# MLP of an encoder: TensorE takes pieces of the second product and half-size products of the first two and two in turn instead of one and one

## The chip, the core and the metric

The kernel runs on one core of a Trainium2 chip. The metric is the device time of one execution, in microseconds; the median of three runs of the kernel before is 1327.92 us (1327.11 to 1327.92). Engines are named as the profile names them: PE is the matrix engine (PEld its loading of weights), DVE the vector engine, ACT the scalar engine, POOL the general engine, SP the one that issues most transfers.

## What is computed

Two layers of an encoder over 512 tokens of 1024 features, in float32. Each layer is a token mixer (a gated delta rule in the first, gated linear attention in the second), a residual layer norm, and then the MLP, which the change is about:

```python
def _sq_relu_mlp(h, w1, w2):
    a = jax.nn.relu(jnp.matmul(h, w1))
    return jnp.matmul(a * a, w2)

x = _layernorm(DEEPNORM_ALPHA * x + m.astype(x.dtype), ln1_g[i], ln1_b[i])
x = _layernorm(DEEPNORM_ALPHA * x + _sq_relu_mlp(x, mlp_w1[i], mlp_w2[i]).astype(x.dtype), ln2_g[i], ln2_b[i])
```

`w1` is 1024 x 4096 and `w2` 4096 x 1024.

## The kernel before

**Arithmetic.** A float32 operand is split into a high part (`h`: a cast on ACT, line 102) and the rest (`l`: a subtraction on DVE, line 107). One product of two tiles is then three matmuls, high by high, high by rest and rest by high (`mm3`, lines 125 to 130). Both products of the MLP use a Winograd form of Strassen's scheme, with seven products of half size in place of eight, and sums of quarters around them.

**The loops.** `mlp` goes over the 4096 hidden features in four groups. While PE works on the second product of group `gi` (`second`, line 564), it also works out the first product of group `gi + 1` (`stream`, line 740). There are three such stretches in each of the two MLPs, six in all.

- A **piece** is a quarter of one of the seven products in `second`: six matmuls of 128x512 into one of the banks pX, pY, pZ (`chunks`, line 544). There are 28 in a stretch, `i` = 0 to 27.
- A **half-size product** belongs to a pair of hidden features (`Pair`, line 450): twelve matmuls of 128x256. A pair has seven, four pairs (`p` = 0 to 3) make 28 in a stretch.

The seven of a pair stand in the order of `products` (line 491), named here by the bank that they write and the number of the product: X1, Z2, X6, Y5, X7, Y3, X4. X is the tile `fx`; Z and Y are the two halves of the tile `fyz`. X is written four times by one pair, and each time its content has to be taken out first: after X1 by ACT (line 499), after X6 by ACT (505), after X7 by DVE (511), after X4 by ACT (520). X4 adds to X, so it waits for line 511 of its pair.

**Weights of a pair.** Its tiles `wh` and `wl` come from rings of three buffers. `prepare(i + 1)`, called when Y5 of pair `i` has been issued (line 749), makes on DVE what products 1, 2 and 5 of the next pair need: a split (ACT 102, DVE 107) in the buffer that Y5 gives back, five sums (DVE, line 464), and a split of half a tile (ACT 470, DVE 471) in the buffer that Y3 gives back. `late` makes the other two splits.

**What sets the order.** On PE the order is that in which the code issues (`in_order`, line 765). On ACT and DVE the framework's scheduler decides at build time, by durations of its own, in which order the instructions of all these helpers stand; on the chip each of these queues is a fixed list, and an instruction that waits holds up those behind it.

The loop that mixes the two kinds is lines 766 to 769: after piece `i` PE takes half-size products until `i + 1` of them have been issued, so one after each piece. In the last stretch of an MLP (`m = 24`), whose pieces 24 to 27 are left for the end, all that is left of the 28 follows piece 23.

Of the kernel before, what the change touches and what calls it, by code (L numbers as in the profile page):

```python
# [351 lines left out]
def mlp(c, w1, w2, g, b, out=None, extra=None, room=0):  # L352
# [14 lines left out]
    with c.banks(pj=2, X=2, Y=2, Z=2), tc.tile_pool(name="mlp", bufs=2) as pool:  # L367
# [51 lines left out]
        def new_h():  # L419
            return [pool.tile([P, HF, S], F32, name="h", tag="h", bufs=3) for _ in range(2)]  # L420
# [143 lines left out]
        def second(gi, h, a):  # L564

            a11, a12, a21, a22 = quarters(h)
            tags = "ZX" if gi + 2 == G else "XZ"
            X, Y, Z = banks(tags[0]), banks("Y"), None
            load(gi, 1, 0)

            def upto(i):

                if i == 5:
                    V.tensor_tensor(a21, a22, a21, ALU.subtract)
                elif i == 6:
                    V.scalar_tensor_tensor(a11, a21, -1.0, a11, ALU.mult, ALU.subtract)
                elif i == 7:
                    V.scalar_tensor_tensor(a21, a11, -1.0, a22, ALU.mult, ALU.subtract)
                elif i == 3:
                    V.scalar_tensor_tensor(a12, a12, -1.0, a11, ALU.mult, ALU.subtract)  # L580
                b = pair({2: a12, 5: a21, 6: a11, 7: a21, 3: a12, 4: a22}[i])
                split(i)
                return b

            steps = ((1, 2, 0, 0, ALU.add, None), (2, 5, 0, 0, ALU.add, None), (5, 6, 2, 1, ALU.subtract, None),
                     (6, 7, 0, 1, ALU.subtract, (0, 0)), (7, 3, 2, 1, ALU.subtract, (0, 1)),
                     (3, 4, 0, 1, ALU.subtract, (1, 1)), (4, None, 2, 0, ALU.add, None))
            for i, nx, t, hf, op, more in steps:
                if i == 2:
                    Z = banks(tags[1])  # L590
                bk = Z if i == 2 else Y if i in (5, 3) else X
                for n, _ in enumerate(chunks(bk, a, i, i in (1, 2, 5))):
                    if n == 0 and nx:
                        b = upto(nx)
                    if n == 3:
                        for j in range(2):
                            add(t + j, hf, bk[j], op)
                        if more:
                            load(gi + 1, *more)
                    yield  # L600
                a = b
# [138 lines left out]
        def stream(gi, nh):  # L740

            for p in range(GF // 2):
                i = (gi - 1) * (GF // 2) + p
                for n, _ in enumerate(ready[i].products(nh)):
                    if n == 0:
                        begin(i + 1)
                    elif n == 1:
                        ready[i].late(1, (7, 3))
                    elif n == 3:
                        prepare(i + 1)  # L750
                    elif n == 5:
                        finish(i + 1)
                    if p == 3 and n == 2 and gi + 1 == G:
                        load(gi, 1, 0, c.wst)
                    if p == 3 and n == 2:
                        split(1, None if gi + 1 < G else True)
                        stream.a = pair(quarters(nh)[0])
                    yield

        for gi in range(G - 1):  # L760
            nh = new_h()
            more = stream(gi + 1, nh)
            n, k = 28, 0
            m = 24 if gi + 2 == G else 28
            with c.in_order(mybir.EngineType.PE):
                for i, _ in enumerate(second(gi, h, a)):
                    while k < n and (k < i + 1 or i + 1 == m):
                        next(more, None)
                        k += 1
                for _ in more:  # L770
                    pass
            h, a = nh, stream.a
# [1040 lines left out]
def body(tc, nc, a, out):  # L1813
    with contextlib.ExitStack() as es:
        def pool(name, bufs, **kw):
            return es.enter_context(tc.tile_pool(name=name, bufs=bufs, **kw))

        c = Ctx(tc, nc, (pool("const", 1), pool("big", 1), pool("wst", 3), pool("whl", 3), pool("small", 4)))
        x = a["x"][0]
        gdn(c, (a["a_in"], a["a_gates"]), a["a_conv"][0], a["a_alog"][0], a["a_dt_bias"][0], a["a_norm_g"][0],  # L1820
            a["a_out"], a["ln1_g"][0], a["ln1_b"][0], x, a["xt"], a["w1_0"])
        with tc.tile_pool(name="gcst", bufs=1) as gp:
            gc = []
            mlp(c, a["w1_0"], a["w2_0"], a["ln2_g"][0], a["ln2_b"][0],
                room=32, extra=lambda tmp: gc.append(GlaConst(c, gp, a["b_gate_b"][0], a["b_norm_g"][0], tmp)))
            gla(c, gc[0], (a["b_in"], a["b_vr"], a["b_gates"]), a["b_gate_w2"][0], a["b_out"], a["ln1_g"][1], a["ln1_b"][1], a["w1_1"])
        mlp(c, a["w1_1"], a["w2_1"], a["ln2_g"][1], a["ln2_b"][1], out=out[0])
# [18 lines left out]
```

## Time and profile before

| | us |
|---|---|
| median of three runs | 1327.92 |
| the profiled execution | 1328.52 |
| span of its trace, first to last instruction | 1326.6 |
| PE busy | 1307.4 |
| DVE busy | 1107.7 |
| ACT busy | 805.2 |
| POOL busy | 124.8 |

The stretches in which pieces and half-size products take turns lie at about 467 to 696 us and 1042 to 1271 us of the span. In the quoted rows of a timeline the columns are start, duration, engine, line, operation, out<-in by the program's names, shape, and in brackets how long the engine had been idle before it and what ended that. Start-to-start distances, not durations, say how fast an engine works through its list, since the end of one instruction overlaps the start of the next.

### The profile page before, as it was taken

How to read it: one execution, taken by the hardware profiler on the slowest of the kernel's cores; microseconds unless marked ns; L12 is line 12 of the kernel's file. 1: busy time of each engine (PE TensorE's matmuls, PEld its weight loads, DVE VectorE, ACT ScalarE, POOL GpSimd, SP SyncE). 2: the span in 40 equal slices, each digit the busy share in tenths (PEclk: the TensorE clock that was granted, in tenths of full speed). 3: DMA queues.
4: the chain of work that ended last, by engine and by line, in shares of the span. 5: the costliest groups of instructions: out<-in, count | busy, mean ns of one | idle time of the engine just before them, and what ended most of it. 6: DMA issues, size and time to landing. Idle time of an engine off the chain costs nothing.

```text
span 1326.6 us, 22309 instructions
## 1 busy us (share of the span) xinstructions
PE 1307.4 (99%) x8659; PEld 1113.2 (84%) x8659; DVE 1107.7 (83%) x1823; ACT 805.2 (61%) x1598; POOL 124.8 (9%) x177
## 2 busy tenths in 40 slices
PE   9999999999999999999999999999999999999996
PEld 7777877787777889999998888888889889999985
DVE  7787888888668988989988787967879789989887
ACT  4757666767643666566667754654456466666656
POOL 5000000000000910101102200000001001101021
PEclk9999999999999999999999999999999999999998
DMA  5210120211222585675648521111216465657465
GB/s 181 96 49 33 49 65 33 64 49 57 73 99 85 189 178 154 156 191 153 151 150 170 149 90 64 65 63 64 95 64 213 105 193 154 149 172 161 142 143 143
DMA packets 44045, 154.36 MB, mean 116 GB/s; under 512 B 5419, under 2 KB 5795, under 8 KB 43939
## 3 DMA queue, kind: packets, MB, share of 16 engines
q1 hardware_dynamic: 32163, 110.85, 24.9%
q0 software_dynamic: 11776, 42.08, 16.1%
q8 instruction: 68, 1.11, 0.3%
q14 instruction: 38, 0.31, 0.1%
HBM read 113.99 MB, written 2.10 MB: 88 GB/s over the span
## 4 chain that ended last, share of the span: by engine, by line
PE 92%; ACT 3%; DVE 3%; issue 1%; DVEq 0%; POOL 0%; ACTq 0%; POOLq 0%
PE fx L128 3%; PE fx L130 3%; PE fx L129 3%; PE pX L130 3%; PE pX L129 3%; PE pX L128 3%; PE pjv L128 3%; PE pjv L129 3%; PE pjv L130 3%; PE m L1708 3%; PE fyz L128 3%; PE fyz L129 3%; PE fyz L130 3%; PE pY L129 2%; PE pY L128 2%; PE pY L130 2%
## 5 line engine op out<-in xcount | busy, mean ns | idle before, releaser
L102 ACT CAST wh<-wst 128x1024 fp32r<-128x1024 f32 x152 | 159.4, 1049 | 110.3 <-PE fyz L129 35.3
L107 DVE TENSOR_TENSOR wl<-wst,wh 128x1024 fp32r<-128x1024 f32 x150 | 184.3, 1229 | 42.2 <-ACT wh L102 41.9
L107 DVE TENSOR_TENSOR w2l<-w2r,w2h 128x1024 fp32r<-128x1024 f32 x92 | 112.3, 1221 | 24.0 <-ACT w2h L102 23.8
L102 ACT CAST w2h<-w2r 128x1024 fp32r<-128x1024 f32 x94 | 98.5, 1048 | 47.4 <-PE pX L130 16.2
L415 POOL DMA_DIRECT2D w2r<-w2r x56 | 48.5, 892 | 493.9 <-DVE w2l L107 247.3
L102 ACT CAST ah<-h 128x1024 fp32r<-128x1024 f32 x56 | 58.9, 1052 | 40.8 <-PE pX L129 18.1
L464 DVE TENSOR_TENSOR wst<-wst 128x512 f32<-128x512 f32 x120 | 79.8, 685 | 0.4
L107 DVE TENSOR_TENSOR al<-h,ah 128x1024 fp32r<-128x1024 f32 x56 | 68.3, 1220 | 5.1 <-ACT ah L102 4.8
L130 PE MATMUL pX<-w2h,al 128*128 128x512 f32 x168 | 66.2, 394 | 0.0
L129 PE MATMUL pX<-w2l,ah 128*128 128x512 f32 x168 | 66.1, 393 | 0.0
L128 PE MATMUL pX<-w2h,ah 128*128 128x512 f32 x168 | 65.8, 392 | 0.0
L128 PE MATMUL pjv<-wh,xth 128*128 128x512 f32 x128 | 54.7, 427 | 0.0
L128 PE MATMUL fx<-xth,wh 128*128 128x256 f32 x192 | 53.6, 279 | 0.0
L130 PE MATMUL fx<-xh,wl 128*128 128x256 f32 x192 | 53.6, 279 | 0.0
L130 PE MATMUL fyz<-xh,wl 128*128 128x256 f32 x192 | 53.6, 279 | 0.0
L128 PE MATMUL fyz<-xh,wh 128*128 128x256 f32 x192 | 53.6, 279 | 0.0
L128 PE MATMUL fx<-xh,wh 128*128 128x256 f32 x192 | 53.5, 278 | 0.0
L129 PE MATMUL fx<-xl,wh 128*128 128x256 f32 x192 | 53.5, 278 | 0.0
L130 PE MATMUL fx<-xth,wl 128*128 128x256 f32 x192 | 53.4, 278 | 0.0
L129 PE MATMUL fx<-xtl,wh 128*128 128x256 f32 x192 | 53.4, 278 | 0.0
L129 PE MATMUL fyz<-xl,wh 128*128 128x256 f32 x192 | 53.4, 278 | 0.0
L129 PE MATMUL pj<-xtl,wh 128*128 128x256 f32 (+1 forms) x160 | 52.0, 326 | 0.2 <-DVE xtl L194 0.2
(538 smaller groups left out, 4320.7 us busy)
## 6 DMA issues: line engine op xcount, KB each, us to landing
wst<-in_w SPq DMA_DIRECT2D x68, 512.0 KB, 4.3
w2r<-in_w SPq DMA_DIRECT2D x60, 512.0 KB, 4.0
w2r<-w2r POOLq DMA_DIRECT2D x56, 512.0 KB, 5.3
wst<-in_a_in SPq DMA_DIRECT2D x32, 512.0 KB, 3.3
wst<-in_b_vr SPq DMA_DIRECT2D x16, 512.0 KB, 3.3
wst<-in_a_out SPq DMA_DIRECT2D x8, 512.0 KB, 3.3
wst<-in_b_in SPq DMA_DIRECT2D x8, 512.0 KB, 3.3
wst<-in_b_out SPq DMA_DIRECT2D x8, 512.0 KB, 3.3
```

Source lines behind the costliest of these rows:

```text
L102: h = nc.scalar.copy(hi, src)
L107: self.halves = h, nc.vector.tensor_tensor(lo, src, hi.bitcast(F32), ALU.subtract)
L128: mm(ps, ah, bh, start=start, stop=False, **kw)
L129: mm(ps, ah, bl, start=False, stop=False, **kw)
L130: self.last_mm = mm(ps, al, bh, start=False, stop=stop, **kw)
L415: nc.gpsimd.dma_start(blocks[a + (q,)], blocks[b + (q,)], accum_op=ALU.add)
L464: plus = lambda a, b: V.tensor_tensor(a, a, b, ALU.add)
L1708: T.matmul(ps[:, d, :], *ops(d), start=True, stop=True)
```

## The change

```diff
             with c.in_order(mybir.EngineType.PE):
                 for i, _ in enumerate(second(gi, h, a)):
-                    while k < n and (k < i + 1 or i + 1 == m):
+                    upto = n if i + 1 == m else i + 1 if i % 7 in (1, 3, 5, 6) else k
+                    while k < upto:
                         next(more, None)
                         k += 1
                 for _ in more:
```

No instruction is added or taken away. After pieces 0, 2 and 4 of every seven no half-size product follows, after 1, 3 and 5 two, after 6 one. With P for a piece, a pair stood on PE as P X1 P Z2 P X6 P Y5 P X7 P Y3 P X4, and now stands as P P X1 Z2 P P X6 Y5 P P X7 Y3 P X4. As the scheduler lays out the other engines around this, the lists of ACT and DVE change too; those of POOL and SP stay as they were.

On DVE, pair `p` = 0 of the second stretch, from the split that waits for Y5 (the first row, `wl`) to the row that takes product 3 out of Y (514). Line 511 takes X7 out of X, 464 are the sums of `prepare`, 471 is the half split that waits for Y3 through its cast on ACT, 576 to 580 are sums for `second`, `w2l` are its weights. Before:

```order
L107 TENSOR_TENSOR wl<-wst,wh 128x1024
L511 TENSOR_TENSOR h<-h,fx 128x256
L464 TENSOR_TENSOR wst<-wst 128x512
L578 SCALAR_TENSOR_TENSOR h<-h 128x4x256
L464 TENSOR_TENSOR wst<-wst 128x512 x2
L471 TENSOR_TENSOR wl<-wst,wh 128x512
L464 TENSOR_TENSOR wst<-wst 128x512 x2
L107 TENSOR_TENSOR w2l<-w2r,w2h 128x1024
L514 TENSOR_TENSOR h<-h,fyz 128x256
```

Now, with the two rows ahead of that split (in the list of before this `w2l` stood there too, and 576 further up):

```order
L107 TENSOR_TENSOR w2l<-w2r,w2h 128x1024
L576 SCALAR_TENSOR_TENSOR h<-h 128x4x256
L107 TENSOR_TENSOR wl<-wst,wh 128x1024
L578 SCALAR_TENSOR_TENSOR h<-h 128x4x256
L464 TENSOR_TENSOR wst<-wst 128x512
L107 TENSOR_TENSOR w2l<-w2r,w2h 128x1024
L464 TENSOR_TENSOR wst<-wst 128x512 x2
L471 TENSOR_TENSOR wl<-wst,wh 128x512
L464 TENSOR_TENSOR wst<-wst 128x512 x2
L511 TENSOR_TENSOR h<-h,fx 128x256
L514 TENSOR_TENSOR h<-h,fyz 128x256
```

Line 511 has moved from the place right behind the split to the place behind 471 and all five sums.

On DVE, pair `p` = 1 of the same stretch, the same section (534 and 536 add a finished piece to the residual `xt`, `al` is the rest of an operand of `second`). Before:

```order
L107 TENSOR_TENSOR wl<-wst,wh 128x1024
L536 TENSOR_TENSOR xt_5508<-xt_5508,pY 128x512
L464 TENSOR_TENSOR wst<-wst 128x512
L511 TENSOR_TENSOR h<-h,fx 128x256
L464 TENSOR_TENSOR wst<-wst 128x512 x2
L107 TENSOR_TENSOR al<-h,ah 128x1024
L464 TENSOR_TENSOR wst<-wst 128x512
L471 TENSOR_TENSOR wl<-wst,wh 128x512
```

Now:

```order
L107 TENSOR_TENSOR wl<-wst,wh 128x1024
L536 TENSOR_TENSOR xt_5508<-xt_5508,pY 128x512
L464 TENSOR_TENSOR wst<-wst 128x512
L107 TENSOR_TENSOR al<-h,ah 128x1024
L464 TENSOR_TENSOR wst<-wst 128x512 x2
L107 TENSOR_TENSOR w2l<-w2r,w2h 128x1024
L471 TENSOR_TENSOR wl<-wst,wh 128x512
L464 TENSOR_TENSOR wst<-wst 128x512 x2
L107 TENSOR_TENSOR w2l<-w2r,w2h 128x1024
L511 TENSOR_TENSOR h<-h,fx 128x256
```

Here 511 has gone from three rows behind the split to the end of the section, behind 471 and two `w2l`. The same two rearrangements stand at `p` = 0 and `p` = 1 of all six stretches (with 578 and 580 for 576 and 578, and 534 for 536, in the first of each MLP). At `p` = 2 and `p` = 3 line 511 stays ahead of 471.

## The prediction

> **What bounds the kernel now.** I read the page's head first, then the busy times of the two stretches that the change touches, then PE's list of waits there, then the timeline of one pair.
>
> ```profile
> span 1326.6 us, 22309 instructions
> PE 1307.4 (99%) x8659; PEld 1113.2 (84%) x8659; DVE 1107.7 (83%) x1823; ACT 805.2 (61%) x1598; POOL 124.8 (9%) x177
> ```
>
> PE is busy for all but 19 us. The view by windows gives for the interleaved stretch of each MLP the window, its length, and the busy time of each engine:
>
> ```profile
> 466.80:696.40 229.60, 229.60 (x1494) 207.88 (x1493) 205.61 (x255) 143.63 (x205) 20.97 (x26) 1.00 0.62 161
> 1041.60:1271.20 229.60, 229.60 (x1494) 207.86 (x1493) 205.22 (x253) 143.05 (x203) 19.30 (x23) 1.00 0.58 155
> ```
>
> PE never stops in these 459 us, and the list of PE's waits is empty for both windows. DVE is second, with 205.61 of 229.60 us, or 90%. So nothing that DVE or ACT do here costs time today, a gain can come only from PE's own pace, and a loss from anything that makes PE wait. DVE has a tenth of its time to spare, but what matters is whether one particular instruction comes in time.
>
> **PE's own pace.** One product, one piece and the next product in the timeline:
>
> ```profile
> 521.17 0.28 PE L128 MATMUL fyz<-xh,wh 128*128 128x256 f32 x1
> ...
> 522.33 0.28 PE L129 MATMUL fyz<-xl,wh 128*128 128x256 f32 x1
> 522.44 0.28 PE L130 MATMUL fyz<-xh,wl 128*128 128x256 f32 x1
> 522.57 0.39 PE L128 MATMUL pY<-w2h,ah 128*128 128x512 f32 x1
> ...
> 523.95 0.28 PE L128 MATMUL fx<-xth,wh 128*128 128x256 f32 x1
> ```
>
> From start to start a product takes 522.57 - 521.17 = 1.40 us and a piece 523.95 - 522.57 = 1.38. The step from the last matmul of a product to the piece is 0.13 us, inside the product it is 0.11 (522.33 to 522.44), so a change of kind costs 0.01 to 0.02 us. A pair had seven of them in each direction and now has four, so 6 x 24 = 144 go. At 0.02 us that is 2.9 us; the rows have two decimals, and I take 0.5. The other direction of the bound: the two neighbours of a longer run may suit each other worse. Products in this trace take between 1.37 us (546.23 to 547.60) and 1.41 (526.72 to 528.13):
>
> ```profile
> 526.72 0.28 PE L128 MATMUL fx<-xth,wh 128*128 128x256 f32 x1
> ...
> 528.13 0.40 PE L128 MATMUL pY<-w2h,ah 128*128 128x512 f32 x1
> ...
> 546.23 0.28 PE L128 MATMUL fx<-xth,wh 128*128 128x256 f32 x1
> ...
> 547.60 0.39 PE L128 MATMUL pX<-w2h,ah 128*128 128x512 f32 x1
> ```
>
> With all 168 at one end, the pace term lies between -5 us (168 x 0.03) and +2 us (168 x 0.01). I take **-0.5 us**.
>
> The Trainium skill (TensorE: Matmul & The Clock Gate, Back-to-back issue gap) gives about 216 ns from start to start for an isolated warm matmul of 512 columns, and no price for a change of size. The rows have 231 ns a matmul (1.38 us / 6), so the measurement decides; by the page the pace term would be 0 instead of -0.5.
>
> **The wait that gets shorter.** All instructions stay, so what counts is distance on PE between an instruction that fills a bank, the one that empties it, and the next one that writes it. For X1 to X6, X6 to X7 and Y5 to Y3 two pieces and a product lie between, before and now. X4 to the next pair's X1 gains a piece. X7 to X4 loses one: from P Y3 P (1.39 + 1.40 + 1.39 = 4.2 us) to Y3 P (2.8 us). In that time DVE has to run line 511. How late that is today, at `p` = 3 of the second stretch, from the piece behind Y5 on:
>
> ```profile
> 536.54 0.40 PE L128 MATMUL pX<-w2h,ah 128*128 128x512 f32 x1
> 536.62 1.05 ACT L102 CAST wh<-wst 128x1024 fp32r<-128x1024 f32 x1 [2.07 <-PE fyz L129]
> 537.70 1.23 DVE L107 TENSOR_TENSOR wl<-wst,wh 128x1024 fp32r<-128x1024 f32 x1 [1.51 <-ACT wh L102]
> 538.96 0.69 DVE L464 TENSOR_TENSOR wst<-wst 128x512 f32<-128x512 f32 x1
> 539.57 1.22 DVE L107 TENSOR_TENSOR w2l<-w2r,w2h 128x1024 fp32r<-128x1024 f32 x1
> 540.71 1.28 DVE L464 TENSOR_TENSOR wst<-wst 128x512 f32<-128x512 f32 x2
> 541.91 0.41 DVE L511 TENSOR_TENSOR h<-h,fx 128x256 f32<-128x256 f32 x1
> 542.24 0.68 DVE L464 TENSOR_TENSOR wst<-wst 128x512 f32<-128x512 f32 x1
> ...
> 543.45 0.28 PE L128 MATMUL fx<-xth,wh 128*128 128x256 f32 x1
> ```
>
> Call 536.54, the end of Y5, S. ACT starts the split at S + 0.08, DVE its half at S + 1.16; 511 ends at 542.32 and X4 starts at 543.45, so 1.1 us is to spare. The steps also give DVE's rate: 1.14 us for an instruction of 1024 columns (539.57 to 540.71), 0.60 for one of 512 (540.71 to 541.91 is two), 0.33 for 511, which itself ends after 0.41.
>
> **Working it for the new lists.** Undisturbed, X4 now starts at S + P P X7 Y3 P = 3 x 1.39 + 2 x 1.40 = S + 6.97.
>
> At **p = 1** DVE is idle when the split arrives: the rows ahead of it are released by pieces that lie before X6 and Y5. Its list from S + 1.16 to 511, as the part on the change shows it: wl 1.14, 536 0.60, 464 0.60, al 1.14, two 464 1.20, w2l 1.14, 471 0.60, two 464 1.20, w2l 1.14, then 511 with 0.41. That is 9.17, so 511 ends at S + 10.33. With some 0.06 us for the signal, X4 starts at S + 10.4 instead of 6.97: PE waits **3.4 us**.
>
> At **p = 0** the two rows ahead of the split push it back. Their chain starts with ACT's `ah`, released by the piece ahead of X6, two products before S, at about S - 2.8; DVE's `al` follows 1.08 later (as 536.62 to 537.70 above), then al, w2l and 576 take 3 x 1.14, so wl starts at S + 1.7. From there wl 1.14, 578 1.14, 464 0.60, w2l 1.14, two 464 1.20, 471 0.60, two 464 1.20, 511 0.41 are 7.43: 511 ends at S + 9.1, and PE waits **2.2 us**.
>
> A floor that does not hang on how busy DVE is: 471 stands ahead of 511 and waits for ACT 470, which waits for Y3.
>
> ```profile
> 542.19 0.62 ACT L470 CAST wh<-wst 128x512 fp32r<-128x512 f32 x1 [3.00 <-PE fyz L129]
> ...
> 542.85 0.41 DVE L514 TENSOR_TENSOR h<-h,fyz 128x256 f32<-128x256 f32 x1
> 543.18 0.68 DVE L471 TENSOR_TENSOR wl<-wst,wh 128x512 fp32r<-128x512 f32 x1
> ```
>
> Y3 is done at about S + 5.6. The cast takes 0.62, 471 0.60, two sums 1.20, 511 0.41: S + 8.5, or 1.6 us late at p = 0, and 2.7 at p = 1 with its second w2l. Before, X4 could never meet this, as 511 stood ahead of 471.
>
> At p = 2 the new list has wl, 536, 464, 536, two 464 and 511: 1.16 + 1.14 + 5 x 0.60 + 0.41 = S + 5.7, in time. At p = 3 the rows are those quoted above, 1.16 + 1.14 + 0.60, then w2l, whose cast waits for the second piece behind S (S + 2.9 and 1.1 for the cast) and so starts at S + 4.0, then 1.14 + 1.20 + 0.41: S + 6.8, just in time, where 1.1 us was to spare. The third stretch of each MLP ends with products alone, before and now.
>
> One more place: where the second stretch of an MLP follows the first, its second piece needs bank X back from the last piece of the first. The distance falls from X4 P X1 to X4 P, and that 536 stands at the end of the list of p = 3, two 464, 514, 471, 536, 464 behind 511: about S + 10.1 against S + 9.76, so 0.35 us, twice.
>
> **Sum.** 6 x (2.2 + 3.4) = 33.6, plus 0.7, minus 0.5: +33.8 us on the profiled execution's 1328.52 (its span and 1.9 us around it), which is 1362.3; that execution lies 0.6 us over the median of the runs, so against the median it is **1362 us**, 2.6% slower. Nothing later wins this back, because PE has no other wait to lose.
>
> **Rivals.**
>
> *Only PE's pace counts (faster).* If DVE ran 511 within the 2.8 us behind X7 at every pair, the change would give what the pace can give, down to -5 us and 1323. It decides for this when 471's cast and the sums end before Y3 and the following piece do, at S + 6.5. Against it stands the floor: 470 cannot start before Y3 ends, and 511 stands behind it in a list that the trace shows run strictly in turn (511 above starts at 541.91, right behind the two sums, though X7, which lies 4.2 us ahead of X4, was done at 539.3).
>
> *The stall is there but small.* If only one of the two places bites, say p = 1 alone at its floor of 2.7, the sum is 16 us less the pace: 1344. If neither does and only the shorter distance counts at p = 3, it is 1329. For it speaks only that 511 has 1.1 us to spare at its worst place today.
>
> *PE's clock falls in the longer waits.* At the end of the kernel PE stops at 1314.60 (last row's start and duration), and the granted clock, the last figure but two of a window's row, goes down:
>
> ```profile
> 1314.20 0.40 PE L130 MATMUL pX<-xh,al 128*128 128x512 f32 x1
> 1317.00:1319.00 2.00, 0.00 (x0) 0.00 (x0) 1.93 (x9) 0.50 (x2) 0.29 (x1) 0.74 1.00 219
> 1319.00:1326.00 7.00, 0.00 (x0) 0.00 (x0) 2.63 (x8) 0.00 (x0) 1.07 (x2) 0.50 0.76 282
> ```
>
> A mean of 0.74 over 1317 to 1319 means half clock from 1317.96, 3.36 us after PE stopped. The wait at p = 1 is 3.4 us by my working, at the edge. If each of the six lost the clock, and it stayed at half for as long as it took to fall, 1.7 us each or 10 us in all would come on top: 1372. The Trainium skill (TensorE: Matmul & The Clock Gate, What's actually happening) has the array at half clock after an idle window of about 3.4 us that runs freely; the row agrees. By that rule a gap of 3.4 us would have to match a window exactly, so few of the six would.
>
> **How the numbers follow.** The forecast has 0.80: two stalls per stretch of the sizes above, each within about 0.6 us, which with the pace gives 1352 to 1370. The clock case has 0.08, the small stall 0.07 (half of it under 1331, so within 0.2%), the faster rival 0.05. A difference of 0.2%, or 2.7 us, is about what a measurement can tell from none. So faster 0.05, the same 0.04, slower 0.91. The range runs from the floors with the best pace (1328.5 + 6 x 4.3 - 5 = 1349) to the clock case: 1349 to 1372.
>
> **What would show it.** In the profile after, PE's list of waits should hold one new row, fx L128 (X4) waiting for DVE h L511, 12 times, about 34 us in total, longest 3.4 to 3.5. DVE's 511 should end just before X4 starts at p = 0 and p = 1, right behind two 464 or a w2l, with 471 ahead of it. The busy time of PE's matmuls should stay within 5 us, and DVE's as it was. The prediction is wrong if that wait isn't there, if 511 overtakes 471, or if products and pieces change their pace by more than 0.03 us each.

## The result, and the profile after

The changed kernel takes **1376.36 us** (median of 4 runs, 1372.32 to 1377.61) against 1327.92 us (1327.11 to 1329.31) for the kernel before on the same chip: a ratio of 1.0358, 95% interval 1.0334 to 1.0383. It is slower, as forecast, but by 48 us and not by 34, and it lies outside the range. The profiled execution took 1377.61 us. The head of its page, and its row in the view by cores (span, mean granted clock):

```profile
span 1375.9 us, 22345 instructions
PE 1324.7 (96%) x8659; PEld 1125.9 (82%) x8659; DVE 1110.1 (81%) x1823; ACT 808.8 (59%) x1598; POOL 125.8 (9%) x177
```

```profile
core 0: 1375.9 us, clock 0.984
```

The same number of matmuls is busy for 17 us longer (1324.7 against 1307.4), and the span is 49.3 us longer. So there are two losses: PE stops, and PE runs slower. The list of PE's waits, first for 460 to 760 us, then for 1040 to 1376 (line waited for, us in total, times, longest):

```profile
PE fx L128 <- DVE h L511: 16.6, 6, 3.3
...
PE fx L128 <- DVE h L511: 16.3, 6, 3.3
```

Both lists hold this one row and no other. It is the forecast's wait, 12 times, **33.0 us**, where 33.6 was worked out. How it comes about at `p` = 1 of the first stretch, in DVE's timeline (start, duration, line, and in brackets the idle time before it):

```profile
502.45 1.22 DVE L107 TENSOR_TENSOR wl<-wst,wh 128x1024 fp32r<-128x1024 f32 x1 [2.23 <-ACT wh L102]
503.59 0.68 DVE L534 SCALAR_TENSOR_TENSOR xt<-xt,pY 128x512 f32<-128x512 f32 x1
504.19 0.68 DVE L464 TENSOR_TENSOR wst<-wst 128x512 f32<-128x512 f32 x1
504.79 1.22 DVE L107 TENSOR_TENSOR al<-h,ah 128x1024 fp32r<-128x1024 f32 x1
505.92 1.28 DVE L464 TENSOR_TENSOR wst<-wst 128x512 f32<-128x512 f32 x2
507.13 1.21 DVE L107 TENSOR_TENSOR w2l<-w2r,w2h 128x1024 fp32r<-128x1024 f32 x1
508.26 0.68 DVE L471 TENSOR_TENSOR wl<-wst,wh 128x512 fp32r<-128x512 f32 x1
508.87 1.28 DVE L464 TENSOR_TENSOR wst<-wst 128x512 f32<-128x512 f32 x2
510.07 1.21 DVE L107 TENSOR_TENSOR w2l<-w2r,w2h 128x1024 fp32r<-128x1024 f32 x1
511.21 0.41 DVE L511 TENSOR_TENSOR h<-h,fx 128x256 f32<-128x256 f32 x1
```

From `wl` on DVE has no idle time, and 511 is the twelfth instruction of that run. PE's timeline at the same place:

```profile
507.94 0.40 PE L130 MATMUL pX<-w2h,al 128*128 128x512 f32 x1
511.67 0.39 PE L128 MATMUL fx<-xth,wh 128*128 128x256 f32 x1 [3.33 <-DVE h L511]
...
512.24 0.35 PE L129 MATMUL fx<-xtl,wh 128*128 128x256 f32 x1
512.39 0.42 PE L130 MATMUL fx<-xth,wl 128*128 128x256 f32 x1
512.60 0.42 PE L128 MATMUL fx<-xth,wh 128*128 128x256 f32 x1
512.82 0.42 PE L129 MATMUL fx<-xtl,wh 128*128 128x256 f32 x1
...
514.32 0.63 PE L129 MATMUL pX<-w2l,ah 128*128 128x512 f32 x1
514.74 0.63 PE L130 MATMUL pX<-w2h,al 128*128 128x512 f32 x1
```

PE stands for 3.33 us. Then, 0.6 us after it has started again, its steps double: from 0.12 us to 0.21 and 0.22 for 256 columns, and 0.42 for 512 columns (514.32 to 514.74) where 0.23 is usual. The view by windows shows the same for both MLPs (window, its length, busy time of each engine; the last but two is the granted clock, 1.00 in both stretches before):

```profile
466.80:720.00 253.20, 236.56 (x1466) 212.41 (x1465) 203.23 (x249) 144.78 (x202) 20.08 (x24) 0.95 0.54 142
1060.00:1320.00 260.00, 243.69 (x1524) 218.58 (x1523) 209.60 (x259) 146.80 (x206) 19.33 (x23) 0.97 0.52 137
```

The trace's record of the clock has ten falls to one half ahead of the kernel's end. Nine last for 3.41 us and one for twice that. At half clock, 11 x 3.41 us less 1.2 us in which PE stood anyway cost half of their length, **18.2 us**. With the waits that is 51.2 us on a span that grew by 49.3, so the pace of PE gave back some 2 us.

The falls begin on a raster of 3.413 us, a fixed grid in time, whatever PE does at that moment. Windows laid on this raster (idle time of PE is a window's length less the first busy time):

```profile
594.22:597.64 3.42, 0.74 (x4) 0.27 (x2) 3.42 (x5) 1.04 (x1) 0.00 (x0) 1.00 0.46 151
597.64:601.05 3.41, 2.75 (x13) 2.75 (x14) 0.93 (x3) 1.26 (x3) 0.00 (x0) 0.50 0.49 159
601.05:604.46 3.41, 3.41 (x10) 2.64 (x10) 1.86 (x2) 1.96 (x3) 0.00 (x0) 0.50 0.10 16
604.46:607.88 3.42, 3.42 (x27) 3.25 (x26) 2.18 (x4) 2.27 (x3) 0.00 (x0) 1.00 0.42 143
1085.74:1089.15 3.41, 1.52 (x8) 0.91 (x6) 3.41 (x7) 0.62 (x1) 1.75 (x2) 1.00 0.51 98
1089.15:1092.57 3.42, 3.20 (x20) 2.90 (x21) 1.63 (x4) 2.86 (x5) 0.00 (x0) 1.00 1.10 210
485.00:488.41 3.41, 1.35 (x11) 1.35 (x12) 2.94 (x6) 1.01 (x2) 0.34 (x1) 1.00 1.08 204
488.41:491.82 3.41, 3.41 (x11) 2.74 (x10) 1.58 (x2) 2.37 (x4) 0.18 (x1) 0.50 0.57 108
```

A window with 2.68 us idle (594.22) is followed by half clock, and so is one with only 2.06 us idle (485.00); one with 1.89 us idle (1085.74) is not. The window at 597.64 is at half clock and has 0.66 us idle: the next is at half clock too. After a busy one (601.05) the clock is back. All six gaps at `p` = 1 lost the clock, and four of the six at `p` = 0, which are only 2.1 to 2.5 us long.

The theory to be tested had three parts: the wait comes from the place of 511 in DVE's list and from the rows put ahead of it; the slower clock comes from PE's idle time in the waits, about 2 us of a window being enough; and apart from these two the order of two and two saves some 2 us. The rivals: the shorter distance on PE makes the stall whatever the list is, and the clock falls for another reason than idleness, such as a heavier load.

### The profile page after: what moved, and what is told of

It reads as the page before. It is cut to its first block, busy times and chain, and to the rows that moved or that the text cites. A ratio compares the mean times of both kernels' runs of the same rounds, so it can differ in the third digit from the quotient of the medians.

```text
span 1375.9 us, 22345 instructions
## 1 busy us (share of the span) xinstructions
PE 1324.7 (96%) x8659; PEld 1125.9 (82%) x8659; DVE 1110.1 (81%) x1823; ACT 808.8 (59%) x1598; POOL 125.8 (9%) x177
## 3 DMA queue, kind: packets, MB, share of 16 engines
q0 software_dynamic: 11776, 42.08, 15.5%
## 5 line engine op out<-in xcount | busy, mean ns | idle before, releaser
L128 PE MATMUL fx<-xth,wh 128*128 128x256 f32 x192 | 58.8, 306 | 33.0 <-DVE h L511 33.0
L128 PEld LDWEIGHTS fx<-xth,wh 128*128 128x128 f32 x192 | 39.6, 206 | 40.0 <-DVE h L511 38.7
L130 PE MATMUL fx<-xth,wl 128*128 128x256 f32 x192 | 57.9, 301 | 0.0
L129 PE MATMUL fx<-xtl,wh 128*128 128x256 f32 x192 | 57.7, 300 | 0.0
```

The costliest lines, as they stand in the source:

```text
L128: mm(ps, ah, bh, start=start, stop=False, **kw)
L129: mm(ps, ah, bl, start=False, stop=False, **kw)
L130: self.last_mm = mm(ps, al, bh, start=False, stop=stop, **kw)
```

## The experiments

Times before are from the same chip in the same job: 1327.72 us for e1 to e4, 1328.06 for e5 to e8, 1328.24 for e9 and e10, 1327.84 for e11.

### 511 ahead again, with PE's order of two and two

In e1 the next pair's splits and sums are issued behind the sum of X7; in e2 the same is done to the kernel before.

```diff
-                    elif n == 3:
+                    elif n == 4:
                         prepare(i + 1)
```

> The changed kernel, with the next pair's splits and sums issued one place later in the program, behind the sum of X7 (L511), so that L511 stands ahead of them in DVE's list at every pair; PE's order is that of two and two. If the order of DVE's list is the cause of both the stall and the fallen clock: no row of PE waiting for L511, granted clock 1.00 in both stretches, and what is left is the gain in pace of some 2.5 us: 1325 us (1323 to 1328). If the stall comes from the shorter distance on PE between X7 and X4 whatever stands in DVE's list (X7's sum or its bank simply come too late): the 12 waits stay, at 1 us or more each, and the time is above 1345 us. If the clock falls for another reason than the idle time of PE: windows at half clock stay with no wait beside them, about 1345 us.

> The kernel before, one and one, with the same move of the splits and sums behind L511. Both theories: no wait of PE in either, so 1328 us within 2. If it is below 1326, the move alone brings what e1 gains, and the order of two and two brings nothing; if e1 is 2 us or more below this one, that is the pace of two and two.

e1 took **1324.19 us** (1323.7 to 1324.75), a ratio of 0.9973 [0.9963, 0.9983] to the kernel before: faster than both kernels. e2 took 1326.63 us (1325.94 to 1327.29), 0.9993 [0.9984, 1.0001], which isn't told apart from no change. DVE's timeline of e1 at the place shown above:

```profile
497.37 1.23 DVE L107 TENSOR_TENSOR wl<-wst,wh 128x1024 fp32r<-128x1024 f32 x1 [2.23 <-ACT wh L102]
498.51 0.68 DVE L534 SCALAR_TENSOR_TENSOR xt<-xt,pY 128x512 f32<-128x512 f32 x1
499.11 1.22 DVE L107 TENSOR_TENSOR al<-h,ah 128x1024 fp32r<-128x1024 f32 x1
500.24 1.22 DVE L107 TENSOR_TENSOR w2l<-w2r,w2h 128x1024 fp32r<-128x1024 f32 x1
501.38 0.42 DVE L511 TENSOR_TENSOR h<-h,fx 128x256 f32<-128x256 f32 x1
501.71 0.69 DVE L464 TENSOR_TENSOR wst<-wst 128x512 f32<-128x512 f32 x1
```

Five sums, 471 and a `w2l` now stand behind 511, which ends 4.43 us after `wl` began and not 9.17. The windows of both MLPs:

```profile
466.80:720.00 253.20, 253.20 (x1604) 227.66 (x1603) 225.91 (x277) 160.13 (x225) 26.22 (x32) 1.00 0.64 163
1040.00:1320.00 280.00, 270.74 (x1678) 241.50 (x1676) 247.76 (x332) 176.40 (x271) 30.15 (x37) 0.99 0.60 154
```

PE never stops in the first; in the second it stops only at the kernel's end, and the record of the clock has no fall ahead of that. No row waits for 511. With the same order on PE the whole loss is gone, so neither the shorter distance nor a heavier load makes it. e1 less e2 is 2.4 us: the pace of two and two. PE's rows of the two traces add up to the same: from start to start, the matmuls of the pieces and of the half-size products take 503.2 us in e2 and 500.7 us in e1, with 324 and 188 changes of kind. That is 18 ns for each of the 136 that go.

### 511 behind, with PE's order of one and one

```diff
-                V.tensor_tensor(h1[:, r], h1[:, r], X, ALU.add)
+                behind = ready.get((self.gi - 1) * (GF // 2) + self.p + 1) if self.p < 2 else None
+                with tc.issue_after(behind.made.ins) if behind else contextlib.nullcontext():
+                    V.tensor_tensor(h1[:, r], h1[:, r], X, ALU.add)
```

(`made` is the last 464 of the next pair.)

> The kernel before, one and one on PE, but with L511 put behind the last of the next pair's sums (L464, which stand behind L471) in DVE's list at p = 0 and p = 1, as the change put it. If the place of L511 in DVE's list is the cause: PE waits for DVE h L511 about 12 times, some 1.7 us at p = 0 and 2.3 at p = 1, about 24 us in all, and some of them take the clock with them: 1350 to 1362 us. If the cause is PE's order of two and two with its shorter distance from X7 to X4: this kernel still has 4.2 us there, no wait, 1328 to 1331 us.

This kernel, e3, took 1371.82 us (1370.92 to 1374.12), a ratio of 1.0336 [1.032, 1.0352], above the 1350 to 1362 that were expected. The page's group of X4's first matmuls (total, mean ns | idle time before them):

```profile
L128 PE MATMUL fx<-xth,wh 128*128 128x256 f32 x192 | 58.1, 302 | 29.7 <-DVE h L513 29.7
```

L513 is that kernel's 511. PE waits for it 12 times, 29.7 us where 24 was worked out: 2.4 to 3.0 us at `p` = 0, where 1.7 was expected, and 2.2 us at `p` = 1, where 2.3 was. Why `p` = 0 is so much longer was not followed up. The record has 8 windows at half clock, 13.3 us. The edit sets the place of one instruction; the scheduler shifted some 30 other rows of DVE's 1823 with it. So the kernel before, with PE's order untouched, becomes nearly as slow as the changed one once 511 stands behind the next pair's sums. PE's new order is not needed for the stall.

### Two and two in some pairs only

```diff
-                    upto = n if i + 1 == m else i + 1 if i % 7 in (1, 3, 5, 6) else k
+                    upto = n if i + 1 == m else i + 1 if i < 14 or i % 7 in (1, 3, 5, 6) else k
```

(e4; with `i >= 7` two and two remains in pair 0 alone, e7, and with `i // 7 != 1` in pair 1 alone, e8.)

> Two and two on PE only in pairs 2 and 3 of each stretch, one and one in pairs 0 and 1. If the stall needs the lists of p = 0 and p = 1: no wait for L511, clock 1.00, and half of the gain in pace: 1327 us (1325 to 1328). If the shorter distance alone makes the stall: 6 to 12 waits at p = 2 and p = 3, above 1335 us.

> Two and two on PE only in pair 0 of each stretch. Six waits for L511 of 2.1 to 2.5 us, 13 us. If such a gap takes the clock with it in most places (2 us of a window are enough): 4 to 6 windows at half clock, 1.7 us each, so 1328 + 13 + 7 to 10 - 1, 1347 to 1351 us. If only a gap as long as a whole window (3.4 us) does: no window, 1340 us (1339 to 1342).

> Two and two on PE only in pair 1 of each stretch. Six waits for L511 of 3.3 us, 20 us. If 2 us of a window are enough: every gap takes at least one window, 6 or 7, so 1328 + 20 + 10 to 12 - 1, 1357 to 1360 us. If a gap must cover a whole window: none or one, 1347 us (1346 to 1350).

e4 took 1325.8 us (1325.14 to 1326.39), 0.9986 [0.9977, 0.9995]: no wait and no fall. The shorter distance costs nothing at `p` = 2 and `p` = 3, where 511 stands ahead of 471. e7 took 1347.94 us (1346.93 to 1349.35) and e8 1360.3 us (1358.91 to 1360.45), 0.3 us above what was expected. The group of X4 in e7, then in e8:

```profile
L128 PE MATMUL fx<-xth,wh 128*128 128x256 f32 x192 | 55.9, 291 | 12.9 <-DVE h L511 12.9
```

```profile
L128 PE MATMUL fx<-xth,wh 128*128 128x256 f32 x192 | 57.5, 300 | 20.5 <-DVE h L511 20.5
```

e7 has 6 waits, 12.9 us, and five of them, none over 2.5 us, lose the clock: 8.5 us. e8 has 20.5 us of waits and 6 falls, two of which last for two windows: 12.2 us. A gap doesn't have to be as long as a window. By the rule that it must, e7 would have taken 1340 us and e8 1347.

### PE kept busy in the gaps

e5 and e6 put matmuls ahead of X4 that write into the half Z, which had been emptied (18 and 28 of them at `p` = 0 and 1 in e5, 6 and 17 in e6).

```diff
                 yield
+                (wd, _), sd = self.w[4]
+                for _ in range({0: 18, 1: 28}.get(self.p, 0)):
+                    T.matmul(Z, wd[:, sd, :][:, 0, :], xa[4][0][:, 0, :], start=False, stop=False, skip_group_check=True)
                 self.mm(X, 4, False)
```

> The changed kernel with PE kept busy in its gaps: ahead of X4, 18 more matmuls of 256 columns at p = 0 and 28 at p = 1 (0.113 us each, so 2.0 and 3.2 us), which add into a half of a bank that was emptied already and that nobody reads again before it is started anew, so the output is unchanged. DVE's list stays as in the changed kernel. If the 33 us of wait and the fallen clock are two things, the second caused by PE's idleness: X4 starts as late as it did, but the clock stays at 1.00: 1328 + 33 - 2.5, 1359 us (1357 to 1362). If the clock falls for another reason than PE's idleness: 1374 to 1378 as before the fill. If the fill itself delayed DVE or X4: above 1378.

> The same with fewer matmuls, 6 at p = 0 and 17 at p = 1, which leaves some 1.4 us of idle PE in each of the 12 places. If a window of 3.41 us loses the next one's clock only when about 2 us of it are idle, as the changed kernel's record has it: no window at half clock, 1359 us (1357 to 1362), the same as with the gaps filled. If every stop of over a microsecond brings it: about 10 windows, 1372 to 1378 us.

Both missed: 1411.29 us (1410.8 to 1412.73) and 1394.94 us (1393.65 to 1396.04). The page's group of the added matmuls in e5 tells why:

```profile
L520 PE MATMUL fyz<-xth,wh 128*128 128x256 f32 x276 | 50.1, 358 | 36.8 <-DVE h L514 36.8
```

Z and Y are halves of one tile, so these matmuls waited for 514, which reads Y and stands right behind 511. They filled no gap but came after it and pushed X4 further back. As a test of the clock these two say nothing beyond their own gaps. e9 and e10 mend it: the target is the bank that the pieces on either side of X4 are filling, and the operand is zeros.

```diff
+                for _ in range({0: 18, 1: 28}.get(self.p, 0)):
+                    T.matmul(chunks.bank[:, :HT], self.w[4][0][0][:, self.w[4][1], :][:, 0, :], zero,
+                             start=False, stop=False, skip_group_check=True)
                 self.mm(X, 4, False)
...
-            for q, j in order:
+            for n, (q, j) in enumerate(order):
+                chunks.bank = bk[order[(n + 1) % 4][1]]
...
+        zero = pool.tile([P, HT], F32R, name="zero", tag="zero", bufs=1)
+        V.tensor_tensor(zero, h[0][:, 0, :HT], h[0][:, 0, :HT], ALU.subtract)
```

> The changed kernel with PE kept busy in its gaps ahead of X4 by matmuls that wait for nothing: 18 of 256 columns at p = 0 and 28 at p = 1 (0.113 us each, 2.0 and 3.2 us) with an operand of zeros, added into the bank that the pieces on either side of X4 are filling, so the output is unchanged; one subtraction more on DVE at each MLP's start makes the zeros. If the clock falls because PE is idle for about 2 us of a window: X4 starts as late as it did, the clock stays at 1.00, and the time is 1328 + 33 - 2.5, 1359 us (1357 to 1362). If the clock falls for another reason: 1372 to 1378 us.

> The same with 6 matmuls at p = 0 and 17 at p = 1, which leaves some 1.4 us of idle PE in each of the 12 places, under the 1.9 us of a window that separate the falls from the others in the runs so far. By that bound no window at half clock, 1359 us (1357 to 1362), as with the gaps filled. If any stop of over a microsecond brings a fall: about 10 windows, 1372 to 1378 us.

e9 took **1360.87 us** (1360.35 to 1361.51) and e10 **1361.24 us** (1361.13 to 1361.63). The group of X4 in e9, then in e10:

```profile
L128 PE MATMUL fx<-xth,wh 128*128 128x256 f32 x192 | 54.8, 285 | 0.3
```

```profile
L128 PE MATMUL fx<-xth,wh 128*128 128x256 f32 x192 | 54.8, 285 | 16.5 <-DVE h L511 16.5
```

Neither has a fall of the clock ahead of the kernel's end. But for the two subtractions that make the zeros, their lists on DVE and ACT are row by row those of the changed kernel. In e9 X4 still starts 2.3 and 3.5 us after the first added matmul, so the stall is all there, but PE is busy in it, and the kernel is 15.5 us faster than the changed one. In e10 PE stands in all 12 places, for up to 1.5 us, and keeps its clock. This sets the two losses apart: some 15.5 us are the clock's, and PE's idle time takes it away.

### How much of the list holds 511 back

In e11 only ACT 470, DVE 471 and the two sums after it are issued behind the sum of X7 (a function `rest` holds them).

```diff
                     elif n == 3:
                         prepare(i + 1)
+                    elif n == 4:
+                        if i + 1 in ready:
+                            ready[i + 1].rest()
```

> The changed kernel with only the last of the next pair's work behind L511: the half split (ACT 470, DVE 471) and the two sums after it; the split wl, the sums ahead of 471 and the w2l stay ahead of L511. If the stall is the sum of all the rows put ahead of L511, each by its duration: p = 0 loses 471 and two sums, 1.8 us, and has 0.4 us left, p = 1 also loses the second w2l, 2.9 us, and has 0.5 left: 12 waits, 5 us, none of them long enough for the clock, 1328 + 5 - 2.5, 1331 us (1328 to 1333). If 471's wait for Y3 is all there is to it: no wait, 1324 to 1326 us. If the rows ahead of 471 are what counts: waits as long as before, 1345 us or more.

This kernel, e11, took 1331.65 us (1331.26 to 1332.67), a ratio of 1.003 [1.0017, 1.0042]. The group of X4, whose add is line 516 in this kernel:

```profile
L128 PE MATMUL fx<-xth,wh 128*128 128x256 f32 x192 | 54.7, 285 | 4.3 <-DVE h L516 4.3
```

12 waits, none over 0.5 us, 4.3 us in all where 5 was worked out, and no fall. With 471 behind 511 the waits are not gone but shorter by the durations of the rows that left, as worked out. The stall is the sum of the rows ahead of 511, each by its duration, not a single wait of 471.

## Why the prediction was wrong in size and right in kind

**Pace.** Forecast -0.5 us, with -5 to +2 as bounds; e1 less e2 gives -2.4. The working counted 144 changes of kind that go; the traces have 136, since in the last stretch of each MLP all that is left follows piece 23, before and now. The 18 ns for each lie within the 10 to 20 that the working read, but in part by luck, for it put them into the one step where the kind changes. In the trace of e2 that step is only 4 ns longer into a piece (119 ns against 115, the usual step of a product) and 2 ns into a product (233 against 231). The rest lies in the steps behind a change: 119 ns for the third matmul of a product and 115 from the seventh on, 230 to 233 ns for the first steps of a piece and 227 for those further on in a row of pieces. The value taken for the sum was too cautious.

**Stall at `p` = 1.** The forecast's S, the start of the piece behind Y5, and ACT's cast 470 in the timeline of the changed kernel:

```profile
501.29 0.39 PE L128 MATMUL pY<-w2h,ah 128*128 128x512 f32 x1
...
506.91 0.62 ACT L470 CAST wh<-wst 128x512 fp32r<-128x512 f32 x1 [2.27 <-PE fyz L129]
```

S is 501.29, and 511 ends at 511.62, which is S + 10.33, the very figure of the working. PE's idle time is 3.33 us for the forecast's 3.4. The forecast reckoned from start to start, and by that X4 comes 3.50 us late: idle time leaves out the 0.17 us by which the matmul ahead of it would have overlapped it.

**Stall at `p` = 0.** 2.46 us idle in the first stretch and 2.1 in the others, for the forecast's 2.2 (2.62 and 2.3 from start to start). `p` = 2 and `p` = 3 are in time, as worked out, and e4 confirms it.

**The floor by 470 and 471** was sound but never set the end: ACT 470 ends at 507.53 in the stretch above, and 471 starts at 508.26, behind a `w2l`. e11 shows what these rows add by their durations alone.

**The 0.35 us at the change of stretch** did not come. The emptying of bank X and the second piece of the second stretch, in the same timeline:

```profile
553.67 0.68 DVE L534 SCALAR_TENSOR_TENSOR xt<-xt,pX 128x512 f32<-128x512 f32 x1
...
554.89 0.39 PE L128 MATMUL pX<-w2h,ah 128*128 128x512 f32 x1
```

The bank is empty at 554.35, 0.5 us ahead of the piece (line 534 does here what 536 does in the later stretches). The walk down the list was some 0.9 us too long there.

**The sum without the clock was right:** 33.8 us were forecast, and e9, where the stall stands and the clock is kept, takes 32.6 us more than the kernel before (1360.87 against 1328.24). That it came so close is in part luck, as its small errors cancel: from start to start the stalls are 35.0 us and not 33.6, the pace -2.4 and not -0.5, the change of stretch 0 and not 0.7.

**The step that failed** is the price of the clock, which the sum put at nothing and left to a rival: "By that rule a gap of 3.4 us would have to match a window exactly, so few of the six would", its chance of 0.08, and its size of 6 x 1.7 us, which set the upper end of the range at 1372. The working looked at the end of the kernel, where a fall came 3.36 us after PE stopped, took that for the length of stop that is needed, and so left out the six gaps at `p` = 0 and held most of those at `p` = 1, 3.4 us by its own sum, for too short as well. One observation of a long stop cannot tell "3.4 us of idle time" from "some share of a window, and then the next edge of the raster". The runs show the second: 10 falls, 18.2 us. Price and direction of one fall were right; their number was not, and one of them lasted for two windows. The Trainium skill (TensorE: Matmul & The Clock Gate, What's actually happening) names a free-running window of about 3.4 us, and the raster of 3.413 us agrees; its condition of an idle window, taken as a wholly idle one, is what the measurements contradict, with 2.06 us of 3.41 at 485.00.

With these 18.2 us the account closes on the profiled executions: 1326.6 + 33.0 (waits) + 18.2 (clock) - 2.4 (pace) = 1375.4 us, against a span of 1375.9. A second account goes matmul by matmul against e1, which has the same order on PE and neither loss: of the 54.0 us between the two spans, 35.0 lie in the 12 steps to X4, 17.3 in the steps at half clock, and 1.7 in all others.

**What would show it.** The one new wait and its 12 times were as announced (33.0 us in total for about 34, the longest 3.3 for 3.4 to 3.5), and DVE's busy time changed by 2.4 us. PE's busy time was announced within 5 us and rose by 17.3, which is the half clock: a matmul at half clock counts as busy for longer. That row alone, in the head of the page, would have sent one to the clock.

## What to carry to other kernels

When the order on one engine changes, look for the instruction that another engine must deliver in time and add up what the new order puts ahead of it in *that* engine's list; in the changed kernel the sum of durations gave nearly every stall to within 0.3 us, by idle time or from start to start, though the one for e3 missed by up to 1.3 us at `p` = 0. An order that was slower can be the faster one once the list beside it is mended: here two and two, together with issuing the next pair's preparation one place later, gains 0.27%. And a repeated stop of PE of 2 us must be priced with the clock that it takes along, 1.7 to 2.0 us for each fall in these runs (e7 and e8), or be kept well under that length (up to 1.5 us cost no clock in e10).

## What the runs showed of the clock that was not expected

Twelve profiled executions (the two kernels and e1 to e10) were laid on the raster of 3.413 us that the clock record itself has, with idle time from PE's rows. Of the windows at full clock, leaving out each kernel's end, all 46 that were followed by half clock had at least 1.90 us of idle PE, and all of the some 4600 that were not had at most 1.90. So the bound is 1.90 us here, 56% of a window. At half clock, the 46 windows after which full speed came back had at most 0.52 us idle; the six after which it did not had 0.66 us or more. A gap of 2.1 us costs its clock or not by where it falls on the raster (one at 1258.6 us was cut by an edge into 1.18 and 0.92 us, and nothing fell), and of the changed kernel's own runs the one with the higher mean clock, 0.988, took 1372.32 us and the one with 0.984 1377.61. The ends of matmuls are modelled in the trace, so the bound holds for idle time as the trace counts it.
